# Part of layer 1's modulation as row products on VectorE, the shift inside the differences of h, and four banks at the start of a down projection

## Chip, cores and metric

The kernel runs on one core of a Trainium2 chip. The metric is device microseconds of one execution, as the median of several. Before the change it is 2492.84 us (three runs, 2488.25 to 2493.60).

## What is computed

One inference step of a two-layer network on 128 prompt tokens and 512 sample tokens (640 columns together), in float32. Each layer is a mixer part (recurrence and two kinds of attention) and a gated convolutional FFN, each behind an adaptive normalization:

```
m = jax.nn.silu(cond) @ w_mod + b_mod          # 1024 -> 6 x 1024, for both conditions
sh1, sc1, g1, sh2, sc2, g2 = split(m, 6)
modulate(x, g, sh, sc) = rmsnorm(x, g) * (1 + sc) + sh
conv_ffn(h): gate, val = split(h @ w_up, 2)    # 2 x 2816 wide
             gate = dwconv(gate, conv_w, conv_b, 1)      # width 3, along the tokens
             return (gelu(gate) * val) @ w_down
layer:  mix = token_mixers(modulate(x, norm1_g, sh1, sc1))
        x = x + g1 * mix
        x = x + g2 * conv_ffn(modulate(x, norm2_g, sh2, sc2))
```

The prompt tokens use one condition vector, the sample tokens the other, so each of the six parts of m (v = 0 to 5 in the kernel, 8 chunks of 128 channels each) has two columns per chunk.

## The kernel before

Activations lie channel by channel: a chunk is 128 channels (partitions) by 640 columns, handled as two halves of 320. Each float32 product is three matmuls, of a high and a low part on either side (`mm3`; tiles wh and wl are the weights' parts, r the activations' or the FFN's hidden values, K2 holds more weight parts). TensorE (PE) is given its work in an order that is written by hand: generators (streams) yield pieces with a time, and the streams' own clocks say which goes next. The other engines' instructions are ordered by a list scheduler by due time and priority (`soon` raises it, MLOW = -200 lowers it). An engine then works through its own list strictly in that order.

PSUM has eight banks here: three G banks (g0, g1, g2), two TB banks (tb0, tb1), PV, and the two halves of S.

**The FFN** (`ffn`, about 740 to 1300 us in layer 0 and 1995 to 2487 us in layer 1). Its 22 hidden chunks go in five groups (0 to 4, 5 to 8, 9 to 12, 13 to 16, 17 to 21). Each group is computed and then multiplied down at once (`staggered`, called a down below), and adds to x by eight residuals of two halves each (`residual`, L1348).

The first three chunks (PLAIN = 3) are plain: gates by `first` (three G banks, one per chunk, half by half), values by `gemm`. The other 19 are done by `pair`, a Strassen-like scheme that gets the gate and value of one chunk from seven products of 12 matmuls of 320 columns on the halves of h: products 1, 6, 7, 5, 4, 2, 3, each in one of six banks in turn (`pair_banks`), each emptied by a VectorE addition (L1537). The order ends so: after product 4 the gate is known, and ScalarE and VectorE run the convolution and GeLU (`ffn_gelu`, L1467 to L1473); after products 2 and 3 the value is, and the chunk's hidden values are gate times value (L1559), rounded on ScalarE (L755) with the rest taken on VectorE (L756), over 640 columns at once. The weights' sums for the next pair are made meanwhile (`pair_weights`, L1495 and L1496 on GpSimd (POOL), L1508 on ScalarE, L1509 on VectorE).

The seven products need differences of h's blocks. `sums_of_h` makes them: ScalarE adds the shift to the kept, not yet shifted blocks (L679, 24 instructions), then GpSimd makes eight differences of 128 x 640 (L684).

**A down's lead.** The first two chunks of a down (m = 0, 1) have their weights made early (`lead_weights`) and are computed by `gemms`: three jobs (m0 half 0, m0 half 1, m1 half 0) on the three G banks, first all hidden chunks but the last, then the last; then the fourth job alone. The last hidden chunk is the one that the preceding pair has just finished, so for a group of four the lead has 27 matmuls before it needs that chunk.

**The modulation.** `mod_stream` runs beside the FFN of layer 0. `mods` computes part v on TensorE: for v = 0 and 3 it does 16 chunks (v and v + 1), for v = 2 and 5 eight chunks; per block of the weight it has matmuls of 512 columns (16 chunks) or 256 columns (8 chunks) with the conditions as weights, accumulated in S, then transposes. In layer 0's FFN it does `mods(1, 0)`, `(1, 2)`, `(1, 3)`, `(1, 5)`, one in each of the downs 0 to 3. `mods_rows` computes a chunk on VectorE instead: a multiply over 128 x 1024 with a summed output (L575, SCALAR_TENSOR_TENSOR), one for each of the two conditions. Before, it runs earlier in the program, beside the attention of layer 0 (16 instructions), not in the FFN.

## Time and profile before

| | |
|---|---|
| median of three runs | 2492.84 us (2488.25 to 2493.60) |
| the profiled execution's own time | 2489.04 us |
| its span on the core | 2487.0 us |
| TensorE busy | 2391.0 us (96%), 16725 matmuls |
| VectorE busy | 1810.3 us (73%) |
| ScalarE busy | 1095.3 us (44%) |
| GpSimd busy | 291.2 us (12%) |
| mean granted TensorE clock | 0.983 of full speed |

The profile is of one execution. A row of its timeline gives the start, the duration of a run of like instructions and, in brackets, how long the engine had been idle and which instruction of which engine released it. The granted clock is what the chip let TensorE run at; where it is halved, the same matmuls lie twice as far apart. TensorE's busy share is high everywhere, so what remains to be read are the places where it waits or runs slowly, and what it executes that could be elsewhere.

### The profile page before, as it was taken

The page shows a single profiled execution, that of the slowest core. Times are in us where ns is not written, and L with a number is a line of the kernel's source. Part 1 is how long each engine was busy: PE and PEld are TensorE (multiplying, and loading weights), DVE is VectorE, ACT ScalarE, POOL GpSimd, SP SyncE. Part 2 cuts the span into 40 slices and gives each one's busy share as a digit, 9 for nine tenths or more (in the row PEclk, how much of TensorE's full clock was granted, in tenths as well). Part 3 has the DMA queues.
Part 4 walks back from the last instruction along what each step waited for, and adds up shares of the span by engine and source line. Part 5 has one row for each costly group of instructions (what it writes and reads, how often), then busy time and mean ns, then how long its engine had stood idle before and what let it go on. Part 6 is the DMA issues. An engine that isn't in the chain of part 4 may idle for free. (4 is left out here: it accounts for less than half of the span.)

```text
span 2487.0 us, 43303 instructions
## 1 busy us (share of the span) xinstructions
PE 2391.0 (96%) x16725; PEld 2268.8 (91%) x16725; DVE 1810.3 (73%) x3439; ACT 1095.3 (44%) x2177; POOL 291.2 (12%) x358
## 2 busy tenths in 40 slices
PE   8999999999997999989999999999999989999998
PEld 8899999988997887968999999999989979999997
DVE  6588787756857556847875688787667568977886
ACT  4246666623335332423443375656233363433443
POOL 0000000000003131422400000000000023432340
PEclk9999999999999999999999999999999989999999
DMA  8752222222633646365342422223225414444433
GB/s 295 240 163 81 72 78 82 92 66 75 215 112 122 215 158 206 125 233 190 108 131 91 137 71 82 76 80 96 64 75 176 156 61 140 128 140 157 136 110 98
DMA packets 158093, 319.23 MB, mean 128 GB/s; under 512 B 16176, under 2 KB 49472, under 8 KB 157888
## 3 DMA queue, kind: packets, MB, share of 16 engines
q1 hardware_dynamic: 157888, 316.47, 39.5%
q8 instruction: 132, 2.16, 0.4%
q14 instruction: 73, 0.60, 0.1%
HBM read 262.12 MB, written 54.29 MB: 127 GB/s over the span
## 5 line engine op out<-in xcount | busy, mean ns | idle before, releaser
L275 PE MATMUL g<-r,wh 128*128 128x320 f32 (+1 forms) x5736 | 1305.7, 316 | 25.6 <-ACT wh L298 8.5
L275 PEld LDWEIGHTS g<-r,wh 128*128 128x128 f32 x5736 | 959.8, 190 | 67.4 <-issue 35.7
L275 PE MATMUL g<-r,wl 128*128 128x320 f32 (+1 forms) x2868 | 892.8, 311 | 3.4 <-DVE wl L301 3.4
L275 PEld LDWEIGHTS g<-r,wl 128*128 128x128 f32 x2868 | 544.5, 190 | 6.0 <-DVE wl L301 6.0
L275 PE MATMUL g<-r,k 128*128 128x320 f32 (+2 forms) x1520 | 265.9, 321 | 33.8 <-DVE f L1537 13.5
L301 DVE TENSOR_TENSOR wl<-wr,wh 128x1024 fp32r<-128x1024 f32 (+2 forms) x227 | 232.2, 1024 | 90.0 <-ACT wh L298 84.1
L275 PEld LDWEIGHTS g<-r,k 128*128 128x128 f32 x1520 | 239.9, 197 | 42.6 <-DVE f L1537 14.5
L1348 DVE SCALAR_TENSOR_TENSOR f<-g,mod,f 128x128 f32<-128x128 f32 (+3 forms) x288 | 115.1, 436 | 185.6 <-PE g L275 153.3
L298 ACT CAST wh<-wr 128x512 fp32r<-128x512 f32 (+2 forms) x137 | 106.8, 784 | 245.3 <-PE g L275 140.9
L1451 POOL MEMSET f<- 128x1 f32 x132 | 12.0, 102 | 1279.6 <-DVE r L756 353.0
L987 DVE TENSOR_REDUCE sm<-s 128x1 f32<-128x640 f32 (+3 forms) x104 | 92.9, 894 | 88.1 <-PE s L275 87.6
L275 PE MATMUL g<-r 128*128 128x322 f32 (+2 forms) x628 | 125.6, 320 | 6.5 <-DVE f L1348 5.0
L756 DVE TENSOR_TENSOR r<-f,r 128x640 fp32r<-128x640 f32 (+2 forms) x110 | 105.6, 965 | 31.8 <-ACT r L755 23.7
L755 ACT CAST r<-f 128x640 fp32r<-128x640 f32 (+2 forms) x110 | 78.8, 723 | 90.9 <-PE s L275 27.0
L275 PEld LDWEIGHTS g<-r 128*128 128x128 f32 x628 | 101.6, 194 | 11.2 <-DVE f L1348 5.6
L1508 ACT CAST wh<-f 128x512 fp32r<-128x512 f32 x116 | 70.2, 617 | 90.7 <-PE g L275 71.5
L275 PE MATMUL g<-wh,r 128*128 128x256 f32 x576 | 107.5, 282 | 0.0
L1469 DVE SCALAR_TENSOR_TENSOR f<-f,vec 128x641 f32<-128x641 f32 x88 | 103.6, 1186 | 3.2 <-ACT f L1467 3.1
L1509 DVE TENSOR_TENSOR wl<-f,wh 128x512 fp32r<-128x512 f32 x116 | 95.6, 827 | 4.5 <-ACT wh L1508 4.4
L275 PE MATMUL s<-k,r 128*128 128x320 f32 (+3 forms) x448 | 92.5, 326 | 1.0 <-ACT k L883 1.0
L275 PEld LDWEIGHTS g<-wh,r 128*128 128x128 f32 x576 | 90.3, 188 | 3.4 <-issue 3.4
L275 PE MATMUL tb<-r,wh 128*128 128x320 f32 x416 | 92.3, 310 | 0.0
(238 smaller groups left out, 3907.5 us busy)
## 6 DMA issues: line engine op xcount, KB each, us to landing
f<-in_wmod SPq DMA_DIRECT2D x176, 256.0 KB, 4.6
wr<-in_win SPq DMA_DIRECT2D x77, 512.0 KB, 3.4
x_middle<-f SPq DMA_DIRECT2D x80, 320.0 KB, 2.2
f<-x_middle SPq DMA_DIRECT2D x80, 320.0 KB, 3.4
wr<-in_wup SPq DMA_DIRECT2D x44, 512.0 KB, 3.5
f<-in_wup SPq DMA_DIRECT2D x40, 512.0 KB, 3.7
wr<-in_wqkv SPq DMA_DIRECT2D x24, 512.0 KB, 3.7
g_kept<-f SPq DMA_DIRECT2D x32, 320.0 KB, 2.2
```

Source lines behind the costliest of these rows:

```text
L275: self.nc.tensor.matmul(**kw)
L298: nc.scalar.copy(wh[:, :n], raw[:, :n])
L301: self.sub_engine().tensor_tensor(out=wl[:, o : o + c], in0=raw[:, o : o + c], in1=wh[:, o : o + c].bitcast(F32), op=ALU.subtract)
L755: nc.scalar.copy(xh[:, :n], t[:, :n])
L756: (eng or nc.vector).tensor_tensor(out=xl[:, :n], in0=t[:, :n], in1=xh[:, :n].bitcast(F32), op=ALU.subtract)
L987: nc.vector.tensor_reduce(out=m_[:, lo:hi], in_=src, axis=AX.XY if hi - lo == 1 else AX.X, op=ALU.max)
L1348: self.nc.vector.scalar_tensor_tensor(out=dst[:, lo:hi], in0=b[:, lo - c0 : hi - c0], scalar=self.mod[:, l, gate + m, i : i + 1], in1=src[ ...
L1451: nc.gpsimd.memset(gp[:, c : c + 1], 0.0)
L1469: nc.vector.scalar_tensor_tensor(out=g[:, :n], in0=gp[:, k : k + n], scalar=fw(k), in1=g[:, :n], op0=ALU.mult, op1=ALU.add)
L1508: self.nc.scalar.copy(h, x)
L1509: self.nc.vector.tensor_tensor(out=lo, in0=x, in1=h.bitcast(F32), op=ALU.subtract)
```

## The change

1. Of layer 1's modulation, v = 0, 1, 2 (24 chunks) is now done by `mods_rows`: 48 row products of 128 x 1024 on VectorE at low priority (MLOW), written with a pace of 9 us in `mod_stream`. TensorE loses 32 matmuls of 512 columns, 32 of 256 and six transposes. `mods(1, 3)` and `mods(1, 5)` stay on TensorE, but are spread with a pace of 9 and 5 us and are no longer begun by a down. The weight DMAs on SyncE's queue go from 144 to 96 of one kind (wmod) and from 8 to 32 of the other (wmodt).
2. `sums_of_h` takes the kept blocks without their shift, and folds the shift into 24 VectorE instructions for each layer (a difference of two shifts is made once, `dsh`). The 24 ScalarE and eight GpSimd instructions go. The modulated chunks of the FFN are also queued in turn (`issue_after`).
3. The third weight of the FFN's first step gets a higher priority (`soon` in `wload`).
4. `gemms` takes as many of the six pair banks as it has jobs, the oldest first, so a lead is four jobs at once: m0 half 0, m1 half 0, m0 half 1, m1 half 1.
5. A group's last pair forms its hidden values half by half (`gated`).

```diff
...
     SUMS, FILL = 2, (0, 0, 4, 0, 0, 0, 0, 0)
-    MLOW, AFTER, PACE = -200, 8, (3.0, 2.0, 3.0, 3.5)
+    MLOW, AFTER, PACE = -200, 8, (3.0, 2.0, 3.0, 9.0)
     CUT, PRE = 1, (False, False)
...
         self.lam = mk([P, DEPTH, 16], F32, "lam")
+        self.dsh = mk([P, 2, 4], F32, "dsh")
         self.ssq = mk([P, NB, 10], F32, "ssq")
...
 
-    def wload(self, src, place=None):
+    def wload(self, src, place=None, soon=None):
         nc = self.nc
         nc.sync.dma_start(out=raw[:, :n], in_=src)
-        with self.soon(self.WSOON) if self.WSOON else nullcontext():
+        with self.soon(soon or self.WSOON):
             if self.h_on_dve and self.L_H:
...
 
-        banks = [self.G.popleft() for _ in jobs]
+        banks = [self.pair_banks[i] for i in range(len(jobs))]
+        self.pair_banks.rotate(-len(jobs))
         n = len(xs)
...
                     evac(m, half, b)
-        self.G.extend(banks)
 
...
 
-    def mods(self, l, v, ahead=2):
+    def mods(self, l, v, ahead=2, pace=0):
 
         n = 8 if v % 3 == 2 else 16
-        yield from self.mods_columns(l, 8 * v, n, ahead)
+        yield from self.mods_columns(l, 8 * v, n, ahead, pace or self.PACE[1])
         if n == 16:
...
 
-    def mods_columns(self, l, c0, n, ahead):
+    def mods_columns(self, l, c0, n, ahead, pace):
 
...
                 q_.append(load(k + ahead))
-            yield self.PACE[1]
+            yield pace
         s = self.F.get()
...
             nc.scalar.activation(out=xh[:, lo:hi], in_=th, func=AF.Identity, bias=shift)
-            nc.vector.scalar_tensor_tensor(
+            last = nc.vector.scalar_tensor_tensor(
                 out=xl[:, lo:hi], in0=th, scalar=shift, in1=xh[:, lo:hi].bitcast(F32),
             )
+        return last.ins
 
...
         self.F.put(*self.x)
-        for k in range(KC):
-            for half in range(2):
-                t = self.hf[half, k // 2][:, (k % 2) * H2 : (k % 2 + 1) * H2]
-                for i, lo, hi in self.segments(half):
-                    th = t[:, lo - half * H2 : hi - half * H2]
-                    nc.scalar.activation(out=th, in_=th, func=AF.Identity, bias=self.mod[:, l, 24 + k, i : i + 1])
+        d = self.dsh
+        s0, s1 = (self.mod[:, l, 24:32, i] for i in range(2))
+        nc.vector.tensor_tensor(out=d[:, 0], in0=s1[:, :4], in1=s0[:, :4], op=sub)
+        nc.vector.tensor_tensor(out=d[:, 1], in0=s1[:, 4:], in1=s1[:, :4], op=sub)
+
+        def diff(out, a, shift, b):
+            nc.vector.scalar_tensor_tensor(out=out, in0=a, scalar=shift, in1=b, op0=ALU.add, op1=sub)
+
+        for k in range(4):
+            o = (k % 2) * H2
+            b11, b21, b12, b22 = (self.hf[half, k // 2 + 2 * r][:, o : o + H2] for half in range(2) for r in range(2))
+            diff(b11[:, :SEQ], b12[:, :SEQ], d[:, 0, k : k + 1], b11[:, :SEQ])
+            nc.vector.tensor_tensor(out=b11[:, SEQ:], in0=b12[:, SEQ:], in1=b11[:, SEQ:], op=sub)
+            diff(b12, b22, d[:, 1, k : k + 1], b12)
+            diff(b22, b22, s1[:, 4 + k : 5 + k], b11)
+            diff(b21[:, :SEQ], b21[:, :SEQ], s0[:, 4 + k : 5 + k], b22[:, :SEQ])
+            diff(b21[:, SEQ:], b21[:, SEQ:], s1[:, 4 + k : 5 + k], b22[:, SEQ:])
         self.hsum = {}
             b11, b21, b12, b22 = (self.hf[half, g + 2 * r] for half in range(2) for r in range(2))
-            for out, in0, in1 in ((b11, b12, b11), (b12, b22, b12), (b22, b22, b11), (b21, b21, b22)):
-                self.sum_engine.tensor_tensor(out=out[:, :T], in0=in0[:, :T], in1=in1[:, :T], op=sub)
             for n, b in ((5, b11), (6, b22), (7, b12), (4, b21)):
...
                 self.hf = {}
+            lasts = []
             for k in range(KC):
...
                 t = self.hf[half, k // 2][:, (k % 2) * H2 : (k % 2 + 1) * H2]
-                with self.soon(self.MSOON):
-                    self.modulated(l, w, k, half, t, half * H2)
+                with self.soon(self.MSOON), self.tc.issue_after(lasts[-2]) if k > 1 else nullcontext():
+                    lasts.append(self.modulated(l, w, k, half, t, half * H2))
             self.mark(name, l, w, half)
...
             cs = [chunk(m) for m in range(n0)]
-            jobs = [(m, half) for m in range(n0) for half in range(2)]
+            jobs = [(m, half) for half in range(2) for m in range(n0)]
 
...
 
-            yield from self.gemms([(m, half, lead[m]) for m, half in jobs[:3]], xs, evac)
-            yield from self.gemms([(m, half, lead[m]) for m, half in jobs[3:]], xs, evac)
+            yield from self.gemms([(m, half, lead[m]) for m, half in jobs], xs, evac)
             if done is not None:
...
         self.ffn_gelu(l, j, gp)
+        xh, xl = self.R.get(), self.R.get()
+
+        def gated(lo, hi):
+            nc.vector.tensor_tensor(out=gp[:, lo:hi], in0=gp[:, lo:hi], in1=ab[:, lo:hi], op=ALU.mult)
+            nc.scalar.copy(xh[:, lo:hi], gp[:, lo:hi])
+            nc.vector.tensor_tensor(out=xl[:, lo:hi], in0=gp[:, lo:hi], in1=xh[:, lo:hi].bitcast(F32), op=ALU.subtract)
+
         add(a, a, (yield from self.product(2, ws, then)))
+        if then is None:
+            with self.soon():
+                gated(0, H2)
         add(b, b, (yield from self.product(3, ws, then)))
-        nc.vector.tensor_tensor(out=gp[:, :T], in0=gp[:, :T], in1=ab[:, :T], op=ALU.mult)
-        self.F.put(ab)
-        self.halves(gp, gv)
+        if then is None:
+            with self.soon():
+                gated(H2, T)
+        else:
+            gated(0, T)
+        self.F.put(ab, gp)
+        gv.append((xh, xl))
 
...
         gates = [self.ffn_gate() for j in range(PLAIN)]
-        ws = self.wide + [self.wload(io["wup"][l, 2])]
+        ws = self.wide + [self.wload(io["wup"][l, 2], soon=2 * self.MSOON)]
         self.cut = self.CUT2
...
         yield from self.mods(0, 5)
-        for g, v in ((0, 0), (1, 2), (2, 3), (3, 5)):
-            yield ("down", 0, g), 0
-            yield from self.mods(1, v)
+        self.get_cond()
+        for v in range(3):
+            yield from self.mods_rows(1, v, self.PACE[3], 1)
+        self.F.put(*self.cb)
+        yield from self.mods(1, 3, 1, 9.0)
+        yield from self.mods(1, 5, 1, 5.0)
 
...
```

The order on TensorE at the third lead of layer 1 (the end of pair 12 and the start of down 2; k2 is a lead weight, r_62 the hidden values), before:

```order
L275 MATMUL g1_72<-r_62,k2_68 128x320 x9
L275 MATMUL g2_73<-r_62,k2_68 128x320 x9
L275 MATMUL g0_71<-r_62,k2_68 128x320 x9
L275 MATMUL g1_72<-r_62,k2_68 128x320 x3
L275 MATMUL g2_73<-r_62,k2_68 128x320 x3
L275 MATMUL g0_71<-r_62,k2_68 128x320 x3
L275 MATMUL g1_72<-r_62,k2_68 128x320 x12
```

and with the change:

```order
L276 MATMUL g0_71<-r_62,k2_68 128x320 x9
L276 MATMUL g1_72<-r_62,k2_68 128x320 x9
L276 MATMUL g2_73<-r_62,k2_68 128x320 x9
L276 MATMUL tb0_75<-r_62,k2_68 128x320 x9
L276 MATMUL g0_71<-r_62,k2_68 128x320 x3
L276 MATMUL g1_72<-r_62,k2_68 128x320 x3
L276 MATMUL g2_73<-r_62,k2_68 128x320 x3
L276 MATMUL tb0_75<-r_62,k2_68 128x320 x3
L276 MATMUL g0_71<-r_62,wh0_64 128x320 x2
```

A lead had three banks, all among those last used by a pair's final products; now it has four, beginning with the one used longest ago, and the matmuls ahead of the last hidden chunk go from 27 to 36.

VectorE ahead of the same place (L1469 and then L1480 are the convolution, L1537 and then L1548 the additions that empty a bank, L1559 and then L1571 the gate times value, L756 and then L1573 the low part of the hidden values), before:

```order
L1469 SCALAR_TENSOR_TENSOR f_61<-f_61,vec_81 128x641
L1537 TENSOR_TENSOR f_61<-f_61,g1_72 128x320
L1469 SCALAR_TENSOR_TENSOR f_61<-f_61,vec_81 128x641
L1537 TENSOR_TENSOR f_61<-f_61,tb0_75 128x320
L1509 TENSOR_TENSOR wl0_66<-f_61,wh0_64 128x512
L1559 TENSOR_TENSOR f_61<-f_61 128x640
L1509 TENSOR_TENSOR wl1_67<-f_61,wh1_65 128x512
L756 TENSOR_TENSOR r_62<-f_61,r_62 128x640
L1348 SCALAR_TENSOR_TENSOR f_61<-g1_72,mod_87,f_61 128x128
```

and with the change:

```order
L1480 SCALAR_TENSOR_TENSOR f_61<-f_61,vec_81 128x641
L1548 TENSOR_TENSOR f_61<-f_61,tb1_76 128x320
L1480 SCALAR_TENSOR_TENSOR f_61<-f_61,vec_81 128x641
L1548 TENSOR_TENSOR f_61<-f_61,pv_77 128x320
L1520 TENSOR_TENSOR wl0_66<-f_61,wh0_64 128x512
L1571 TENSOR_TENSOR f_61<-f_61 128x320 x2
L1520 TENSOR_TENSOR wl1_67<-f_61,wh1_65 128x512
L1573 TENSOR_TENSOR r_62<-f_61,r_62 128x320 x2
L1360 SCALAR_TENSOR_TENSOR f_61<-g0_71,mod_87,f_61 128x128
```

The product and the low part are now two instructions of 320 columns each, one directly behind the other.

VectorE at the start of the FFN of layer 0 (L659 and then L660 are h's low parts, L1348 and then L1360 the last residuals of the mixer part, L301 and then L302 the low parts of up weights), before:

```order
L659 SCALAR_TENSOR_TENSOR r_62<-f_61,mod_87,r_62 128x192
L659 SCALAR_TENSOR_TENSOR r_62<-f_61,mod_87,r_62 128x128
L659 SCALAR_TENSOR_TENSOR r_62<-f_61,mod_87,r_62 128x192 x7
L1348 SCALAR_TENSOR_TENSOR f_61<-g1_72,mod_87,f_61 128x320
L1348 SCALAR_TENSOR_TENSOR f_61<-g2_73,mod_87,f_61 128x320
L301 TENSOR_TENSOR wl0_66<-wr_63,wh0_64 128x1024
L607 TENSOR_TENSOR f_61<-f_61 128x320
L301 TENSOR_TENSOR wl1_67<-wr_63,wh1_65 128x1024
```

and with the change:

```order
L660 SCALAR_TENSOR_TENSOR r_62<-f_61,mod_87,r_62 128x192
L655 SCALAR_TENSOR_TENSOR f_61<-f_61,am_88,tb0_75 128x128
L655 SCALAR_TENSOR_TENSOR f_61<-f_61,am_88,tb0_75 128x192
L660 SCALAR_TENSOR_TENSOR r_62<-f_61,mod_87,r_62 128x192
L660 SCALAR_TENSOR_TENSOR r_62<-f_61,mod_87,r_62 128x128
L660 SCALAR_TENSOR_TENSOR r_62<-f_61,mod_87,r_62 128x192
L1360 SCALAR_TENSOR_TENSOR f_61<-g2_73,mod_87,f_61 128x320
L608 TENSOR_TENSOR f_61<-f_61 128x320
L302 TENSOR_TENSOR wl1_67<-wr_63,wh1_65 128x1024
```

The residual that empties g2 stands behind h's whole first half now, and the residual that empties g1 and the low part in wl0 have moved ahead of these rows.

VectorE in the first pair of group 1 of layer 0 (s_74 is the pair of S banks that a row product writes), before:

```order
L1537 TENSOR_TENSOR f_61<-f_61,g0_71 128x128
L1537 TENSOR_TENSOR f_61<-f_61,g0_71 128x192
L1509 TENSOR_TENSOR wl1_67<-wr_63,wh1_65 128x512
L1469 SCALAR_TENSOR_TENSOR f_61<-f_61,vec_81 128x641
L1537 TENSOR_TENSOR f_61<-f_61,g1_72 128x320
L1509 TENSOR_TENSOR wl0_66<-wr_63,wh0_64 128x512
L1469 SCALAR_TENSOR_TENSOR f_61<-f_61,vec_81 128x641
L1537 TENSOR_TENSOR f_61<-f_61,g2_73 128x320
L1509 TENSOR_TENSOR wl1_67<-f_61,wh1_65 128x512
L1559 TENSOR_TENSOR f_61<-f_61 128x640
```

and with the change:

```order
L1548 TENSOR_TENSOR f_61<-f_61,tb1_76 128x128
L1548 TENSOR_TENSOR f_61<-f_61,tb1_76 128x192
L1520 TENSOR_TENSOR wl1_67<-wr_63,wh1_65 128x512
L576 SCALAR_TENSOR_TENSOR s_74,mod_87<-f_61 128x1024
L1548 TENSOR_TENSOR f_61<-f_61,pv_77 128x320
L1520 TENSOR_TENSOR wl0_66<-wr_63,wh0_64 128x512
L1548 TENSOR_TENSOR f_61<-f_61,g0_71 128x320
L1520 TENSOR_TENSOR wl1_67<-f_61,wh1_65 128x512
L1480 SCALAR_TENSOR_TENSOR f_61<-f_61,vec_81 128x641 x2
L1520 TENSOR_TENSOR k2_68<-f_61,k2_68 128x512
L576 SCALAR_TENSOR_TENSOR s_74,mod_87<-f_61 128x1024
```

Two row products stand in this stretch now, among the additions and the weights' low parts. Of the 48 row products 25 stand in the stretches of pairs and 23 in downs.

## Rows read from the trace of the kernel before

**Rows 1.** The page, busy time of TensorE: us, share of the span, instructions.

```profile
PE 2391.0 (96%) x16725; PEld 2268.8 (91%) x16725; DVE 1810.3 (73%) x3439; ACT 1095.3 (44%) x2177; POOL 291.2 (12%) x358
```

**Rows 2.** Busy time by stretch; columns PE, PEld, DVE, ACT, POOL, granted clock, DMA share, GB/s.

```profile
901.00:957.00 56.00, 53.56 (x362) 53.30 (x361) 52.74 (x77) 26.32 (x48) 21.78 (x21) 0.99 0.36 114
...
2211.00:2257.00 46.00, 45.99 (x314) 45.73 (x313) 44.44 (x63) 21.89 (x39) 22.74 (x21) 1.00 0.33 102
2101.00:2130.00 29.00, 29.00 (x200) 29.00 (x199) 16.13 (x29) 6.76 (x11) 6.18 (x8) 1.00 0.49 165
```

**Rows 3.** Groups by form on PE, the modulation: busy and mean ns, idle before.

```profile
L275 PE MATMUL s<-f,cond 128*32 128x512 f32 x192 | 33.2, 620 | 3.2 <-DMA f<-in_wmod 3.2
...
L275 PE MATMUL s<-f,cond 128*32 128x256 f32 x192 | 15.9, 405 | 0.0
...
L279 PE MATMUL s<-ident,f 128*128 128x128 f32 x22 | 4.2, 282 | 2.6 <-ACT f L1739 2.6
```

**Rows 4.** Waits of PE, 870 to 1000 us: us in total, times, longest.

```profile
PE g L275 <- DVE f L1348: 3.8, 1, 3.8
PE g L275 <- ACT wh L298: 2.8, 1, 2.8
...
PE s L275 <- DMA f<-in_wmod: 2.2, 1, 2.2
```

**Rows 5.** Waits of PE, 1060 to 1200 us.

```profile
PE g L275 <- ACT wh L298: 5.2, 2, 2.9
PE g L275 <- DVE f L1348: 3.9, 2, 2.3
```

**Rows 6.** Waits of PE, 2170 to 2450 us.

```profile
PE g L275 <- DVE f L1537: 6.9, 2, 3.5
PE g L275 <- ACT r L755: 3.4, 2, 3.1
```

**Rows 7.** Waits of PE, 940 to 1300 us.

```profile
PE g L275 <- DVE f L1537: 6.5, 2, 3.3
...
PE g L275 <- ACT r L755: 3.6, 2, 2.7
```

**Rows 8.** Timeline of PE: two leads with 48 matmuls each.

```profile
1152.62 7.56 PE L275 MATMUL g<-r,k 128*128 128x320 f32 x48 [3.27 <-DVE f L1537]
...
2343.14 10.09 PE L275 MATMUL g<-r,k 128*128 128x320 f32 x48 [3.47 <-DVE f L1537]
```

**Rows 9.** Timeline, all engines, end of a group's last pair.

```profile
2256.68 0.31 PE L275 MATMUL tb<-r,wl 128*128 128x320 f32 x1
...
2263.78 0.82 DVE L756 TENSOR_TENSOR r<-f,r 128x640 fp32r<-128x640 f32 x1 [0.19 <-ACT r L755]
```

**Rows 10.** Timeline, all engines, start of the FFN of layer 0.

```profile
752.25 1.17 PE L275 MATMUL g<-r 128*128 128x320 f32 x3 [2.51 <-DVE f L1348]
...
772.09 15.09 POOL L684 TENSOR_TENSOR f<-f 128x640 f32<-128x640 f32 x8 [113.85 <-ACT f L679]
...
774.45 7.72 DVE L756 TENSOR_TENSOR r<-f,r 128x640 fp32r<-128x640 f32 x4 [3.39 <-ACT r L755]
...
783.60 1.35 ACT L755 CAST r<-f 128x640 fp32r<-128x640 f32 x2 [3.44 <-POOL f L684]
...
785.32 0.62 PE L275 MATMUL g<-r,wh 128*128 128x320 f32 x2 [4.42 <-ACT f L1458]
```

**Rows 11.** Timeline of DVE beside attention: row products.

```profile
149.29 1.23 DVE L575 SCALAR_TENSOR_TENSOR s<-f 128x1024 f32<-128x1024 f32 x1
...
150.64 1.23 DVE L575 SCALAR_TENSOR_TENSOR s<-f 128x1024 f32<-128x1024 f32 x1
```

**Rows 12.** Timeline, all engines, within a pair of layer 1.

```profile
2223.77 1.81 POOL L1496 TENSOR_TENSOR f<-f 128x512 f32<-128x512 f32 x1
...
2224.32 1.80 DVE L1509 TENSOR_TENSOR k<-f,k 128x512 fp32r<-128x512 f32 x1
...
2227.18 0.68 DVE L1509 TENSOR_TENSOR k<-f,k 128x512 fp32r<-128x512 f32 x1
```

## Prediction

> **What bounds the kernel now.** I read the page first: TensorE is busy 2391.0 of 2487.0 us [rows 1], so less of its work, or less waiting and slow running between its work, shortens the run, and nothing else does. Then the busy times by stretch [rows 2], where the reader is to see two kinds of stretch in the FFN. In a stretch of pairs VectorE is nearly as full as TensorE: 52.74 of 56 us in layer 0 (901 to 957), 44.44 of 46 in layer 1 (2211 to 2257). In a down it is not: 16.13 of 29 us (2101 to 2130, a down of layer 1 in which TensorE never waits). Work given to VectorE is therefore cheap in downs and dear in pairs. Third the waits of TensorE in the FFNs [rows 4 to 7], and fourth the timeline around the longest of them [rows 8 to 10], which tells what each wait hangs on.
>
> A lost microsecond of TensorE is lost slightly more than once: the same 48 matmuls of a lead took 7.56 us behind a wait of 3.27, and 10.09 behind one of 3.47 [rows 8], with the granted clock on its lower level (1.2 of 2.4 GHz) for a while. That is 2.5 us more for one, nothing for the other; I add half a microsecond for each microsecond of a wait of over 2 us.
>
> **The change, part by part**, against the profiled execution's own time, 2489.04 us, which is 3.8 us below the median.
>
> *Work off TensorE.* One of three calls with 512 columns, one of three with 256 and six transposes of 22 leave: 33.2/3 + 15.9/3 + 6 x 4.2/22 = 11.1 + 5.3 + 1.1 = 17.5 us [rows 3]. Matmuls run back to back, so this is on the path: **-17.5**.
>
> *Waits of the downs that they stood in.* Downs 0 and 1 of layer 0 had waits of 3.8, 2.8 and 2.2 us [rows 4], with half as much again 13.2. The like down of layer 1, without modulation, has none [rows 2]. But one row product or another will stand ahead of a residual, so I leave 2: **-11**.
>
> *The two calls that stay* are spread, with a pace of 9 and 5 us for 2, and their loads one ahead. In their downs TensorE waited 5.2 + 3.9 us [rows 5], with the half 13.6. Spreading them takes pressure from the banks that wait for a residual (L1348), not from those that wait for a weight (L298). I take less than half: **-6**, bounds 0 and -13.
>
> *The leads of layer 1.* Three leads wait there, 6.9 + 3.4 = 10.3 us [rows 6], with the half 15.4. Product 3 ends at 2257.0 and the last hidden chunk is whole at 2264.6, 7.6 us later [rows 9]; the wait itself is shorter because 27 matmuls lie between, but it is on an addition (L1537): the lead's oldest bank still held a product that was not yet added. With the oldest of six banks first that wait goes, and 36 matmuls, three quarters of 7.56 us or 5.7 [rows 8], run meanwhile. By halves the first half of the chunk is whole half a microsecond sooner (a cast and a low part over 320 columns for 640, VectorE's 0.82 [rows 9]), so 7.1 - 5.7 = 1.4 us remain, too short to count the half: 3 x 1.4 = 4.2 of 15.4 remain, **-11**, bounds 0 and -15.
>
> *The front of the FFN, in both layers.* TensorE waits 4.42 us at 785.32 for a copy on ScalarE (L1458). The copy is late since ScalarE stands in a cast (L755) that waited 3.44 us for GpSimd's differences (L684), 15.09 us for eight of them; and VectorE's four low parts beside them took 7.72 us [rows 10], 1.93 each against 0.82 [rows 9]. With the differences on VectorE the cast waits no more: 4.4 and the half, 6.6, and about 1 in the small waits behind. The 24 added VectorE instructions are paid by what the low parts get back, 6 x 1.1 us, and by its waits of some 2 us before each. Against that the residual that empties g2 has gone behind all of h's first half, and TensorE already waits 2.51 us for it [rows 10]: some 1.5 us more. Net 6 a layer: **-12**, bounds -4 and -18.
>
> *Row products among pairs.* 25 of the 48 stand there. One takes 150.64 - 149.29 = 1.35 us from start to start [rows 11], so 34 us of work go to an engine with 3 us to spare in 56 [rows 2]. What they can use is the leads' waits of layer 0, 6.5 + 3.6 us [rows 7], with the half 15, which parts 4 and 5 of the change would else give back. So 34 - 15 = **+19**, bounds 0 (low priority does put them where VectorE waits) and +34.
>
> *Row products in downs.* 23 x 1.35 = 31 us into 13 us of idle time in each of four downs [rows 2]; hidden, but for one or two that stand ahead of a residual with a bank behind it: **+3**, bounds 0 and +12. On SyncE's queue 48 loads of 128x512 go and 24 of 128x1024 come, as many bytes, while the DMA engines are a third to a half busy [rows 2]: nothing.
>
> *The sum:* -17.5 - 11 - 6 - 11 - 12 + 19 + 3 = -35.5, so 2453.5 for an execution like the profiled one; I add a little for the median standing above it: **2455 us**.
>
> **Rivals.**
>
> *VectorE and GpSimd block each other.* A low part of 128x512 took 1.80 us beside a GpSimd addition of 1.81, and 0.68 without [rows 12]; it began 0.55 us after the addition and ended 0.54 us after it, as if it had stood still meanwhile. A row product has two inputs of SBUF too, is twice as long, and in a stretch of pairs GpSimd is busy 21.78 of 56 us [rows 2]. If some 21 of the 25 meet one, each loses 0.8 us on average (half of 1.8, less what it would have waited anyway), 17 us: 2472. Against it: no row product of the trace stands beside a GpSimd addition (those of [rows 11] do not), and the 1.35 us of each may end in a wait that VectorE has anyway. The Trainium skill says in "SBUF — State Buffer", section "Who interferes with whom", that a VectorE instruction with two SBUF inputs and a GpSimd instruction that reads SBUF exclude each other, and whichever starts first holds the port for its whole length; the two durations of 0.68 and 1.80 us [rows 12] agree. By that rule the time is this rival's 2472, without it 2455.
>
> *Every wait is gone, the rows hide.* The +19 and +3 fall away and the 12 us left in the other terms go: 2455 - 22 - 12 = 2421. The priority speaks for it, the 94% of VectorE against.
>
> *The halves do not start early.* In VectorE's order the two halves stand directly behind each other, behind the last addition, so the first half is no sooner whole, and TensorE waits as before for the first matmul that needs it; the -11 of layer 1 goes and a third of the 15 of layer 0: 2455 + 16 = 2471. Against it: what the trace names is the bank, not the chunk, and that does go.
>
> *Slower: VectorE has no idle time that counts.* If its order is so strict that each row product delays the chain behind it, in downs too, then 48 x 1.35 = 65 us instead of 22 are on the path, and 24 differences for each layer at some 0.45 us, 22 us, replace the -12: 2455 + 43 + 12 = 2510, or more with the differences in full. It decides from about 40 of the 48 on the path on. Against it stand the 13 idle us in each down.
>
> *No change:* if the TensorE time given up comes back as waits for VectorE, term by term, near 2490.
>
> **How the numbers follow.** The sum's mechanism 55%, blocking ports 15%, halves without effect 12%, all waits gone 8%, slower 6%, no change 4%. The range holds the first four with the sum's own spread (about 15 us to either side): 2426 to 2483. About 0.2%, 5 us, is what a measurement of this kernel can tell from no change. Faster by more: 55 + 15 + 12 + 8 less a tail of 3, 87%; within it 4 and 2 of the tail, 6%; slower 6 and 1, 7%.
>
> **What would show it.** Right: no waits for L1548 at leads of layer 1 and at most 1.5 us for the hidden values; no wait for the copy behind `first`; GpSimd busy only with weights' sums; VectorE full in layer 0's pairs and TensorE waiting there for it, in layer 1's not; layer 1's FFN shorter by about 17 us. Wrong: row products of clearly over 1.23 us beside GpSimd (ports); leads that still wait over 3 us for the hidden values (halves); new waits for L1360 in layer 0's downs of 20 us or more (slower); no waits among the pairs of layer 0 at all (all gone). The prediction fails if the pairs of layer 0 grow by over 34 us or not at all.

## The result, and the profile after

The changed kernel takes 2459.02 us (median of four runs, 2456.83 to 2461.74) against 2491.64 of the kernel before beside it: ratio 0.9871, 95% interval 0.9854 to 0.9888. The forecast was 2455, in a range of 2426 to 2483, faster. The total was right; two of its terms were far off in opposite directions, and that is what most of the runs below are about.

The page's busy times, which answer to [rows 1]:

```profile
span 2457.5 us, 43056 instructions
...
PE 2365.7 (96%) x16591; PEld 2262.5 (92%) x16591; DVE 1871.5 (76%) x3605; ACT 1078.1 (44%) x2137; POOL 264.0 (11%) x342
```

The 134 instructions that TensorE loses are the two calls, 64 instructions each in the profile (two for each of 32 matmuls), and the six transposes.

The span is 29.5 us shorter. How it divides over the layers is read from the last masked attention product of layer 1, at which both kernels do the same work; a tile's matmuls, with the start of the first and the last, before:

```profile
L275 PE MATMUL s<-mask,identb x96: 219/230/233, 501.3 to 1889.2; 128*128 128x128 bf16 x96
```

and after:

```profile
L276 PE MATMUL s<-mask,identb x96: 219/230/233, 502.5 to 1876.4; 128*128 128x128 bf16 x96
```

12.8 us were won before it, which is in the FFN of layer 0, and the other 16.7 behind it, in the FFN of layer 1. Layer 1 has no modulation beside it, and its sum went as forecast (11 for its leads, 6 for its front). The first residual of its first down, before and after, divides it:

```profile
2095.25 1.72 DVE L1348 SCALAR_TENSOR_TENSOR f<-g,mod,f 128x128 f32<-128x128 f32 x5 [0.67 <-PE g L275]
2078.12 0.68 DVE L1360 SCALAR_TENSOR_TENSOR f<-g,mod,f 128x128 f32<-128x128 f32 x2 [1.34 <-PE g L276]
```

From the last masked product to there it is 206.1 us before and 201.7 after, so 4.3 us were won ahead of the downs, the front among it, and 12.4 from there on, where four of the five leads stand. The waits of TensorE around its leads, 2080 to 2430 us, answer to [rows 6]:

```profile
PE g L276 <- ACT r L1572: 1.7, 2, 0.9
...
PE tb L276 <- ACT r L1572: 1.1, 1, 1.1
PE g L276 <- DVE r L1573: 1.0, 2, 0.5
PE tb L276 <- DVE r L1573: 0.5, 1, 0.5
```

The additions (L1537, now L1548) are gone from the list; what is left is the last hidden chunk, 1.7 + 1.1 + 1.0 + 0.5 = 4.3 us (4.2 forecast).

At the front of the FFN the wait for ScalarE's copy [rows 10] is gone in both layers, and the third bank is later, as forecast: 4.3 us for 2.51, 1.8 more where 1.5 were forecast. Waits of TensorE, 740 to 830 us:

```profile
PE g L276 <- DVE f L1360: 5.4, 2, 4.3
```

In layer 0 it looks different. Waits of TensorE, 850 to 1150 us, the stretch of the first four downs, the longest sums:

```profile
PE g L276 <- DVE f L1360: 12.4, 7, 3.6
PE tb L276 <- ACT r L1572: 5.7, 1, 5.7
PE g L276 <- ACT wh L299: 4.0, 2, 2.6
PE g L276 <- ACT f L1555: 3.7, 2, 3.3
PE g L276 <- DVE wl L302: 3.7, 3, 3.3
PE pv L276 <- ACT f L1555: 3.6, 1, 3.6
```

The kernel before had the first and the third of these rows in the same stretch (L1348 with 7.7 us and L298 with 5.2); the others are new or were under half a microsecond. Most lead to VectorE, the ones on L1572 and L1555 by way of ScalarE, whose queue had waited for it. What VectorE itself waited for, 800 to 1150 us:

```profile
DVE s L576 <- DMA f<-in_wmodt: 14.9, 7, 3.7
DVE f L1360 <- PE g L276: 14.8, 11, 4.0
DVE f L1360 <- DMA f<-x_middle: 6.3, 6, 3.4
```

The first row is a row product that stands at the head of VectorE's queue and waits for its weights: 14.9 us, in seven places. Everything that stands behind it in the queue waits too, urgent or not. The worst place is the second lead. VectorE's timeline there:

```profile
933.72 1.23 DVE L576 SCALAR_TENSOR_TENSOR s<-f 128x1024 f32<-128x1024 f32 x1 [2.09 <-DMA f<-in_wmodt]
...
937.26 1.23 DVE L576 SCALAR_TENSOR_TENSOR s<-f 128x1024 f32<-128x1024 f32 x1
```

and TensorE's, with a wait of 5.68 us and then one of 3.09:

```profile
939.44 0.63 PE L276 MATMUL tb<-r,k 128*128 128x320 f32 x1 [5.68 <-ACT r L1572]
...
946.75 0.90 PE L276 MATMUL g<-r,wh 128*128 128x320 f32 x2 [3.09 <-DVE f L1360]
```

Two row products (1.35 us each) and one wait of 2.09 us stand in the chain of the last hidden chunk. By stretch, a stretch of pairs and this down, which answer to [rows 2]:

```profile
890.00:936.00 46.00, 43.55 (x295) 43.02 (x293) 43.88 (x67) 19.62 (x36) 17.70 (x19) 1.00 0.33 104
936.00:966.00 30.00, 21.62 (x120) 20.35 (x120) 21.66 (x44) 5.24 (x10) 0.00 (x0) 0.77 0.69 227
```

In the down TensorE is busy for 21.62 of 30 us, and its granted clock, 0.77 on average, fell to the lower of its two levels behind both waits. Downs were the stretches in which row products were to cost next to nothing.

The row products themselves, by form (16 of the 64 stand beside attention):

```profile
L576 DVE SCALAR_TENSOR_TENSOR s<-f 128x1024 f32<-128x1024 f32 x64 | 90.4, 1412 | 18.6 <-DMA f<-in_wmodt 18.3
```

The mean is 1.41 us where [rows 11] had 1.23: eleven of the 48 took 2.15 to 2.33 us. One of them and the GpSimd additions beside it:

```profile
1017.88 2.33 DVE L576 SCALAR_TENSOR_TENSOR s<-f 128x1024 f32<-128x1024 f32 x1
```

```profile
1017.48 1.63 POOL L1505 TENSOR_TENSOR f<-f 128x512 f32<-128x512 f32 x1
1019.07 2.27 POOL L1506 TENSOR_TENSOR f<-f 128x512 f32<-128x512 f32 x1
```

It began 0.4 us into one addition and ended 1.1 us after that had ended, and the next addition takes 2.27 us in its turn. So the rival of the blocked ports is real; its size is eleven times 1.1 us, 12 us of VectorE (17 were priced). The Trainium skill states such an exclusion in "SBUF — State Buffer", section "Who interferes with whom", and this trace agrees with it: 2.33 us for 1.23.

### The profile page after: what moved, and what is told of

It reads as the page before. It is cut to its first block, busy times and chain, and to the rows that moved or that the text cites. A ratio compares the mean times of both kernels' runs of the same rounds, so it can differ in the third digit from the quotient of the medians.

```text
span 2457.5 us, 43056 instructions
## 1 busy us (share of the span) xinstructions
PE 2365.7 (96%) x16591; PEld 2262.5 (92%) x16591; DVE 1871.5 (76%) x3605; ACT 1078.1 (44%) x2137; POOL 264.0 (11%) x342
## 3 DMA queue, kind: packets, MB, share of 16 engines
q8 instruction: 131, 2.15, 0.4%
## 5 line engine op out<-in xcount | busy, mean ns | idle before, releaser
L302 DVE TENSOR_TENSOR wl<-wr,wh 128x1024 fp32r<-128x1024 f32 (+2 forms) x227 | 232.3, 1023 | 65.4 <-ACT wh L299 60.0
L276 PE MATMUL g<-r,k 128*128 128x320 f32 (+2 forms) x1256 | 220.3, 317 | 17.1 <-ACT r L1572 3.9
L276 PEld LDWEIGHTS g<-r,k 128*128 128x128 f32 x1256 | 196.0, 193 | 24.3 <-ACT r L1572 4.9
L1360 DVE SCALAR_TENSOR_TENSOR f<-g,mod,f 128x192 f32<-128x192 f32 (+3 forms) x258 | 103.8, 435 | 126.8 <-PE g L276 116.4
L276 PE MATMUL tb<-r,k 128*128 128x320 f32 x636 | 104.0, 312 | 8.6 <-ACT r L1572 6.8
L276 PEld LDWEIGHTS tb<-r,k 128*128 128x128 f32 x636 | 96.2, 190 | 11.9 <-ACT r L1572 7.3
L576 DVE SCALAR_TENSOR_TENSOR s<-f 128x1024 f32<-128x1024 f32 x64 | 90.4, 1412 | 18.6 <-DMA f<-in_wmodt 18.3
L1480 DVE SCALAR_TENSOR_TENSOR f<-f,vec 128x641 f32<-128x641 f32 x88 | 99.4, 1137 | 2.6 <-ACT f L1478 2.5
```

Source lines behind the costliest of these rows:

```text
L276: self.nc.tensor.matmul(**kw)
L302: self.sub_engine().tensor_tensor(out=wl[:, o : o + c], in0=raw[:, o : o + c], in1=wh[:, o : o + c].bitcast(F32), op=ALU.subtract)
L576: nc.vector.scalar_tensor_tensor(out=self.S, in0=w.ap, scalar=1.0, in1=self.cb[i].ap, op0=ALU.mult, op1=ALU.mult, accum_out=self.mod[:, l, ...
L1360: self.nc.vector.scalar_tensor_tensor(out=dst[:, lo:hi], in0=b[:, lo - c0 : hi - c0], scalar=self.mod[:, l, gate + m, i : i + 1], in1=src[ ...
L1480: nc.vector.scalar_tensor_tensor(out=g[:, :n], in0=gp[:, k : k + n], scalar=fw(k), in1=g[:, :n], op0=ALU.mult, op1=ALU.add)
```

## Experiments

Each figure is the median of four to six executions. Each group of runs stands beside executions of the kernel before of its own (medians 2487.7 to 2491.6 us), so runs are compared by their ratios; a difference in us is the difference of two ratios times 2490, uncertain by some 6 us. The change has 0.9871.

**The modulation on TensorE again, the rest of the change kept** (`mod_stream`):

```diff
-        self.get_cond()
-        for v in range(3):
-            yield from self.mods_rows(1, v, self.PACE[3], 1)
-        self.F.put(*self.cb)
-        yield from self.mods(1, 3, 1, 9.0)
-        yield from self.mods(1, 5, 1, 5.0)
+        for g, v in ((0, 0), (1, 2), (2, 3), (3, 5)):
+            yield ("down", 0, g), 0
+            yield from self.mods(1, v)
```

> The change with layer 1's modulation wholly on TensorE again, one part in each of downs 0 to 3 of layer 0 as before; parts 2 to 5 stay. Theory A (the sum as predicted: -17.5 -11 -6 +19 +3): part 1 is worth 12.5 us, so this run stands at about 2471 us, 0.992 of before. Theory B (read from the trace of the change: row products that wait for their weights stop VectorE's queue for 14.9 us and ten of them take 2.3 us for 1.23, so that part 1 gives back what it takes from TensorE): 2455 to 2463 us, within 0.2% of the change. If the four calls find the waits of before again in full, 2471 or more.

2457.04 us, ratio 0.9866 (0.9847 to 0.9884). Part 1 of the change, the one that its name begins with, is worth nothing that can be measured (+1 us); parts 2 to 5 are worth all of it, -33. The expectation for theory A was put together wrongly: the 15 us of leads in layer 0 that stand within the +19 belong to parts 4 and 5, so that the prediction's own sum for part 1 is -17.5 - 11 - 6 + 34 + 3 = +2.5, and for the others -11 - 12 - 15 = -38. Read so, it agrees with both numbers, and this run alone does not tell A from B. It does show that part 1 holds a large loss against its large gain; the next runs size both.

**Without the loads, and without the work.** In the first, `mods_rows` loads one weight for eight chunks; in the second each row product covers 16 columns:

```diff
+            if j == 8 * v or not l:
-            w = q.popleft()
+                w = q.popleft()
...
-            self.F.put(w)
-            q.append(load())
+            if not l or j == 8 * v + 7:
+                self.F.put(w)
+            if not l:
+                q.append(load())
```

```diff
+        n = 8 if l else 512
...
-                        out=self.S, in0=w.ap, scalar=1.0, in1=self.cb[i].ap, op0=ALU.mult, op1=ALU.mult,
+                        out=self.S[:, :, :n], in0=w.ap[:, :, :n], scalar=1.0, in1=self.cb[i].ap[:, :, :n], op0=ALU.mult, op1=ALU.mult,
```

> The change with one weight load for each of v = 0, 1, 2 instead of eight: 21 of the 24 loads of layer 1's row products are left out, so three parts of layer 1's modulation are computed from the wrong weights; the 48 row products stay. Theory B: VectorE's 14.9 us of waits for these loads go, and with them the waits of TensorE behind them (5.7 and 3.1 us at 939 and 947, 3.3 and 2.5 at 866 and 877, with slow running some 4 more): 2445 to 2451 us. Theory A: such waits fall into time that VectorE has in the downs anyway: 2457 to 2461 us.

> The change with layer 1's row products over 16 of their 1024 columns (the rest of these sums is left out); all loads stay. Theory A: the price of the rows, +19 among pairs and +3 in downs, is VectorE's time, so it goes: about 2437 us. Theory B: half of it is the wait for the loads, which stays: 2444 to 2452 us.

2436.35 us, ratio 0.9789 (0.9769 to 0.9809), and 2434.27 us, ratio 0.9771 (0.9751 to 0.9791): 20 and 25 us less than the change. The first gains more than theory B had, the second is what theory A had. The loads' waits on VectorE, 800 to 1150 us, without 21 of the 24 loads:

```profile
DVE s L577 <- DMA f<-in_wmodt: 1.5, 1, 1.5
```

and with tiny products:

```profile
DVE s L577 <- DMA f<-in_wmodt: 21.9, 13, 3.6
```

Against a run that has neither loads nor row products (0.9631 with 3 us for an edit of its own, below) the work without the waits still costs some 36 us, the loads with next to no work (0.30 us for each product) 32, both together 57. So neither theory has the whole: the loads, which the prediction priced at nothing, weigh about as much as the work.

The run without the loads also tells where the work costs. Its row products stand elsewhere than the change's, mostly about the downs and mostly singly or in twos, and seven of them, not eleven, took 2.15 us or more. Waits of TensorE behind the leads of downs 0, 1 and 2 (843 to 874, 936 to 966 and 1023 to 1046 us), all of them:

```profile
PE g L276 <- DVE wl L302: 0.9, 1, 0.9
PE g L276 <- DVE f L1363: 1.7, 1, 1.7
PE g L276 <- DVE f L1363: 0.6, 2, 0.4
```

That is 3.2 us, in the second of these stretches with VectorE busy for 28.95 of 30 us; so row products that wait for nothing do find room in a down. What is left of the 36 us stands elsewhere, for the most part at leads and among pairs: TensorE's waits for the last hidden chunk are 9.7 us (800 to 1100 us), for additions 4.8.

**Asked for earlier:**

```diff
-            yield from self.mods_rows(1, v, self.PACE[3], 1)
+            yield from self.mods_rows(1, v, self.PACE[3], 2)
```

> The change with the row products' weights asked for two chunks ahead instead of one. Theory B: the waits for these loads go or halve, 2447 to 2454 us. Rival: the loads are late because the places they go to come free late, or because the queue is behind other loads, so that asking sooner changes nothing: 2457 to 2461 us; or they delay the downs' own weights, over 2462 us.

2467.08 us, ratio 0.9909 (0.9886 to 0.9932): 9 us more than the change. VectorE waits 9.5 us for loads where it waited 14.9, but TensorE, 850 to 1150 us, now waits for residuals:

```profile
PE g L276 <- DVE f L1360: 35.0, 12, 6.3
```

against 12.4 in the change. The row products have moved into the downs, ahead of residuals; that GpSimd, which works among pairs, hardly meets them any more is seen in their mean of 1.25 us, 1.41 in the change:

```profile
L576 DVE SCALAR_TENSOR_TENSOR s<-f 128x1024 f32<-128x1024 f32 x64 | 79.8, 1246 | 13.3 <-DMA f<-in_wmodt 12.8
```

Between 862 and 871 us five stand ahead of a residual with one other instruction among them, where the run without loads has them mostly singly or in twos and TensorE waits 2.3 us for residuals (800 to 1100 us). So asking earlier changed the order of the work along with the loads, and what the earlier load alone would bring is not shown.

**The differences of h on GpSimd, and the leads on three banks.** The first puts the 24 ScalarE and eight GpSimd instructions of `sums_of_h` back in place of the 24 on VectorE, as in the diff of the change. The second:

```diff
-        banks = [self.pair_banks[i] for i in range(len(jobs))]
-        self.pair_banks.rotate(-len(jobs))
+        banks = [self.G.popleft() for _ in jobs]
...
+        self.G.extend(banks)
...
-            jobs = [(m, half) for half in range(2) for m in range(n0)]
+            jobs = [(m, half) for m in range(n0) for half in range(2)]
...
-            yield from self.gemms([(m, half, lead[m]) for m, half in jobs], xs, evac)
+            yield from self.gemms([(m, half, lead[m]) for m, half in jobs[:3]], xs, evac)
+            yield from self.gemms([(m, half, lead[m]) for m, half in jobs[3:]], xs, evac)
```

> The change with the shift added on ScalarE and the eight differences of h on GpSimd again; all else as in the change. Theory A (as predicted, 6 us a layer): about 2471 us. Theory B (waits and slow running at the front of the FFN went from 17.0 to 7.2 us in layer 0 and from 17.7 to 11.4 in layer 1): about 2475 us. Rival: with h queued in turn and the third weight early the front is mended without the moved sums: 2457 to 2463 us.

> The change with three G banks and the old order of jobs at a down's lead; the last pair by halves stays. Theory A: the four leads of layer 1 wait again as before, 11 us, and those of layer 0 up to 10 us: 2470 to 2480 us. Rival: the wait was for the last hidden chunk, which comes by halves now, and not for the bank: 2457 to 2463 us.

2471.18 us, ratio 0.9935 (0.9921 to 0.9949): the moved differences are worth 16 us (12 forecast, bounds 4 and 18). Waits of TensorE at the front of layer 1, 1980 to 2060 us, with them back:

```profile
PE g L276 <- ACT f L1460: 4.6, 1, 4.6
PE g L276 <- ACT f L681: 4.6, 1, 4.6
```

The wait for ScalarE's copy is there again, and the wait in the place of the third bank is now for the shift on ScalarE. The kernel before had no wait for that shift there, so the 16 us are what the moved differences are worth within the change. The gain over the kernel before is smaller: ahead of the downs it is 4.3 us in layer 1 (above) and, in the run with part 1 undone, 8.2 in layer 0 (345.6 us before and 337.4 there, from the first masked product to the first residual), 12.5 together.

2467.28 us, ratio 0.9914 (0.9901 to 0.9928): the four banks are worth 11 us in both layers together, slightly under the lower end of what was expected. In layer 1 the waits for an addition return, 2080 to 2430 us:

```profile
PE g L276 <- DVE f L1549: 6.8, 2, 3.4
PE g L276 <- ACT r L1573: 2.4, 1, 2.4
```

the 6.9 of [rows 6] almost exactly. So the wait was for the bank, and the rival (halves alone) falls.

**The modulation on TensorE, but spread, not in bursts:**

```diff
-        self.get_cond()
-        for v in range(3):
-            yield from self.mods_rows(1, v, self.PACE[3], 1)
-        self.F.put(*self.cb)
-        yield from self.mods(1, 3, 1, 9.0)
-        yield from self.mods(1, 5, 1, 5.0)
+        for v, pace in ((0, 9.0), (2, 9.0), (3, 9.0), (5, 5.0)):
+            yield from self.mods(1, v, 1, pace)
```

> The change with all of layer 1's modulation on TensorE, but spread (a pace of 9, 9, 9 and 5 us, one load ahead, not begun by a down) in place of one part in each down. Theory B: TensorE's 17.5 us come back, but the waits that the row products make in layer 0 (some 37 us and 14 of slow running between 857 and 1145 us) go, and those of a part within a down (some 19 us with the clock) are halved: 2444 to 2452 us. Rival: loads for TensorE's modulation block its order as they did VectorE's, wherever they stand: 2455 to 2462 us.

2418.49 us, ratio 0.9713 (0.9697 to 0.9729): 39 us less than the change, with 134 more matmuls on TensorE, and well outside of what either theory had. TensorE's waits, 850 to 1150 us, are these and no others:

```profile
PE g L276 <- DVE f L1360: 3.0, 3, 1.9
PE g L276 <- ACT r L1572: 0.2, 1, 0.2
```

The run with the parts in bursts differs in when they are done, and in that a part's loads are asked for two blocks of its weight ahead, not one; its row of VectorE's waits, 800 to 1150 us, tells what a burst does:

```profile
DVE f L1360 <- DMA f<-x_middle: 28.8, 8, 9.6
```

and spread it is

```profile
DVE f L1360 <- DMA f<-x_middle: 5.9, 2, 3.1
```

A part of the modulation asks for 32 or 16 loads of 256 KB, 8 or 4 MB, within one down, on the queue that also fetches the chunks of x to which the down's residuals are added. The residuals come late, and with them the banks. The down's own weights come on that queue too, and late as well. The kernel before had both waits (VectorE and ScalarE, 800 to 1200 us):

```profile
DVE f L1348 <- DMA f<-x_middle: 28.2, 8, 9.7
ACT wh L298 <- DMA wr<-in_wdown: 38.1, 3, 16.1
```

The three waits of the second row stand directly ahead of the three of TensorE for that cast in downs 1 to 3 [rows 4, 5]; the burst run has 43.0 us in that row, the spread ones have no such row. ScalarE also stood 37.7 us in the copy that ends a part (L526), waiting for the part's matmuls. Loads and matmuls are spread together here, so that it is the loads is read from the two rows above; no run spreads the one without the other.

**The spread alone, in the kernel before** (the same edit of `mod_stream`, one block ahead for two, and the pace passed on):

> The kernel before with its modulation on TensorE spread by the paces 9, 9, 9 and 5 us, one load ahead, and nothing else of the change. Theory: the waits of the four downs go with their slow running, 13.2 + 13.6 us, in part: 2464 to 2475 us. Rival: the leads of layer 0 and the front still hold everything back, 2480 to 2490 us. If the spread alone is worth what it is beside the other parts (2457 against 2418 us), about 2450 us.

2447.21 us, ratio 0.9826 (0.9809 to 0.9842): 43 us less than the kernel before, more than the whole change brings. TensorE's waits between 800 and 1200 us, all of them:

```profile
PE g L275 <- DVE f L1537: 3.7, 2, 2.4
PE g L275 <- ACT r L755: 0.8, 1, 0.8
PE g L275 <- DVE r L756: 0.4, 1, 0.4
```

The waits of the downs [rows 4, 5] are gone altogether, and about half of those at the leads of layer 0 [rows 7] with them.

**The spread, and residuals first.** To the spread run this is added in `staggered`, for the last chunks ahead of a normalization:

```diff
-                with self.soon():
+                with self.soon(3 * self.SOON if after is not None and half else None):
```

> As the run before it, and the last residuals ahead of an FFN or a layer get a higher priority, so that the one that empties g2 stands ahead of most of h's first half. Theory: the wait of 4.31 us and the slow running behind it (1.8 and 2.7 us) at the front of both FFNs shrink to under 2 us, and those at the start of layer 1 too: 6 to 12 us less than the run before it. Rival: h's low parts come later by as much, and TensorE waits for them: the same within 2 us.

2413.39 us, ratio 0.9700 (0.9687 to 0.9713), the best kernel of this study. The further 3 us, where 6 to 12 were expected, are not clear of noise. In the profile the wait of 4.31 us at the front of layer 0 is gone and one of 3.22 us stands a little later, for a square of VectorE (L608) that was behind it in the queue.

**From there, three more.** Whole hidden chunks (`gated(0, T)` for every pair); parts 0 to 2 of the modulation left out; and v = 2 by row products:

```diff
+        self.get_cond()
+        yield from self.mods_rows(1, 2, 9.0, 1)
+        self.F.put(*self.cb)
-        for v, pace in ((0, 9.0), (2, 9.0), (3, 9.0), (5, 5.0)):
+        for v, pace in ((0, 9.0), (3, 9.0), (5, 5.0)):
             yield from self.mods(1, v, 1, pace)
```

> The run with spread modulation on TensorE and early residuals (2413 us), with the last pair's hidden values formed over 640 columns at once again. Theory: the first half is whole half a microsecond later at eight leads, where TensorE now waits 0.9 us for it at most: 2 to 6 us more, 2415 to 2420 us. Rival: the halves stand directly behind each other in VectorE's order and bring nothing: 2411 to 2415 us.

2422.75 us, ratio 0.9726 (0.9711 to 0.9742): the halves are worth 6 us, at the upper end and just clear of the noise. The wait they shorten is only part of that. The lead at pair 16 of layer 1, whole chunks (TensorE's timeline):

```profile
2284.06 0.41 PE L276 MATMUL g<-r,k 128*128 128x320 f32 x1 [1.46 <-ACT r L1572]
...
2285.32 1.53 PE L276 MATMUL tb<-r,k 128*128 128x320 f32 x6
```

and halves:

```profile
2278.58 0.41 PE L276 MATMUL g<-r,k 128*128 128x320 f32 x1 [0.90 <-ACT r L1572]
...
2279.89 1.05 PE L276 MATMUL tb<-r,k 128*128 128x320 f32 x6
```

Behind 1.46 us the six matmuls take 1.53 us, behind 0.90 they take 1.05. The stretches that begin with these six, whole and then halves (the last column but two is the granted clock):

```profile
2285.30:2288.80 3.50, 3.50 (x17) 3.50 (x16) 2.92 (x8) 1.69 (x3) 0.00 (x0) 0.55 0.24 95
2279.80:2283.30 3.50, 3.50 (x26) 3.50 (x25) 3.25 (x9) 1.66 (x3) 0.00 (x0) 1.00 0.46 162
```

With whole chunks TensorE ran at the lower of its two levels for most of the 3.5 us, with halves at the upper one throughout.

> As the same run, with parts 0, 1 and 2 of layer 1's modulation left out on every engine (constants stand in their place; their loads go too). Theory: on TensorE, spread, they cost what the rows of the kernel before say, 11.1 + 5.3 + 1.1 = 17.5 us, and no wait: 2394 to 2398 us. Rival: their matmuls fill time in which TensorE would wait for a bank: 2400 to 2413 us. This is the least that any way of computing them elsewhere could reach.

2398.46 us, ratio 0.9631 (0.9616 to 0.9647): 17 us less than with them, their loads included. The first term of the prediction, 17.5 us of matmuls and transposes, is what they cost when nothing else goes wrong.

> The run at 2413 us with the eight chunks of v = 2 alone as 16 row products on VectorE (pace 9, one load ahead), v = 0, 1, 3, 4, 5 spread on TensorE. Theory: TensorE gives up 5.3 + 0.4 us, and a row product costs what the 48 of the change cost beside a spread TensorE version, (2459 + 17.5 - 2418) / 48 = 1.2 us each, so 16 cost 19: 2421 to 2431 us. Rival: few row products find room in VectorE's idle time: 2406 to 2411 us.

2426.22 us, ratio 0.9737 (0.9717 to 0.9757): 9 us more than the same part on TensorE, for 5.7 us that TensorE gave up: some 15 us for 16 row products, nearly 1 us each. With an uncertainty of 6 us, few of them are hidden little better than many, if at all (57 us for 48).

## Why the prediction was right, and where it was not

**Right, with their sizes.** The work off TensorE: 17.5 us forecast, 17 measured by leaving it out. The front: 12 forecast, 12.5 found ahead of the downs of both layers, and 16 by moving the differences back; the mechanism is the one named (ScalarE's copy behind a cast behind GpSimd). The leads of layer 1: 4.2 us of waits left forecast, 4.3 found; the bank decides, as the three-bank run shows. The whole of layer 1: 17 us forecast, 16.7 found. Parts 2 to 5 together: 38 by the prediction's working, 33 measured, which is within the noise; by the profile of the run that has them alone (span 2455.1 us, masked products from 499.5 to 1874.3) 17.0 lie in layer 1, where 17 were forecast, and 13.1 in layer 0, where 6 + 15 were. So the 15 us for the leads of layer 0 were too many (banks and halves brought 11 and 6 over both layers, for 26). The blocked ports were given 15% as the main story and are a side one, though the sign that the prediction named for it, row products of clearly over 1.23 us, did show, and so did that for late halves, at one lead of layer 0 (5.68 us). The rival in which halves bring nothing is refuted by 6 us; the slower one by the result.

**Wrong: two terms of part 1, which cancelled.**

*The waits in the downs of layer 0* stood in the sum with -11 and -6, at most -27. Spreading the modulation, one block of loads ahead, and changing nothing else took 38 us from the run with bursts and 43 from the kernel before. The step that failed is the one that read only TensorE's waits in two windows [rows 4, 5], and took it that spreading takes no pressure from the waits for a weight (L298): those, 8.0 us in three places, went with the rest. What lay under them is a wait of ScalarE, 38.1 us for the down's own weights, and under the waits for a residual one of VectorE, 28.2 us for the chunks of x. With them went waits at the leads of layer 0 too, which the prediction had put down to the banks alone. The cause is the burst and not which engine multiplies; that its loads do it, and not its matmuls, is argued from these rows.

*The row products* stood there with +34 and +3, at most +46. By the ratios, the kernel without these parts (0.9631) lies 60 us under the change; 3 of that are the residuals' priority, so some 57 us are the price of the rows. The step that failed is "nothing" for the DMAs. The loads come late in seven places, and in an engine that works through its list in order a low-priority instruction that waits holds up all that are urgent: without 21 of the 24 loads the price is 36 us, near the 37 that the two terms have for the work alone. The other step, "13 us of idle time in each down", held where nothing was waited for (3.2 us of waits in three downs). In the down that it was read from, 2101 to 2130 us, VectorE's idle time is all of one kind:

```profile
DVE f L1348 <- PE g L275: 13.2, 12, 1.5
```

It is in twelve pieces of 1.1 us on average, each ended by TensorE's next product. An instruction of 1.35 us that is ready costs little there; one that stands and waits for its own load is another thing.

38 instead of 17 won, 57 instead of 37 lost: the sum for part 1 was +2.5 and +1 was measured. That the total came out is luck. The sign that the prediction asked for ("the pairs of layer 0 grow") would not have told; only the runs with one part undone show that a right total stood on two wrong terms.

What stays open: what of the 36 us that the work costs without its waits is GpSimd's port and what VectorE's plain time. In the run without loads seven of 48 met the port, some 8 us of VectorE; a run with none was not tried, nor one in which the loads come in time and the products stand where they stood.

## What to carry to other kernels

Before work is moved to an engine because it looks idle, price the transfers that move with it, and not by their bytes alone: an instruction with a transfer of its own in front of it makes the whole in-order queue wait, whatever its priority. And where an engine waits, read what the engine that releases it was waiting for; here two rows of late transfers stood one step behind the waits that were counted. Where a side task's loads come in bursts, spread them before moving its arithmetic; here that alone was worth 43 us, more than the change, and with parts 2 to 5 of the change 71. And undo a change part by part even when its total came out as forecast.

## What the runs showed that was not expected

- The loads of 48 row products cost about as much (32 us with 0.30 us of work for each product) as the products without waiting (36 us).
- A wait of 1.46 us at a lead of layer 1 was followed by 3.5 us at a granted clock of 0.55, one of 0.90 us by none (and one of 3.27 us, in [rows 8], by none either). So some 0.6 us off each of three such waits is not all that the halves brought there, and the prediction, which counted slow running only for waits of over 2 us, had no term for it.
- With the modulation spread, TensorE is busy for 2363.7 us (98% of 2418.6) with 134 matmuls more than the change, which has it busy for 2365.7: the busy time of the page holds the slow running too, and that is what went.
